# A hybrid attention layer: side work pinned behind later instructions, two down-projection tiles interleaved

## The chip, the cores and the metric

The kernel runs on one core of a Trainium2 chip. The metric is device time of one launch in microseconds (us): 954.92 us as the median of three runs before the change (954.69 to 955.83). Engines are named as in the profile: PE is TensorE (matmuls, transposes), DVE is VectorE, ACT is ScalarE, POOL is GpSimd, SP is SyncE. Here SP issues the weight loads, POOL the loads and stores of the new tokens' work, and ACT two small stores. TensorE's clock has two levels, 1.2 and 2.4 GHz; the profile shows the granted one as 0.50 and 1.00.

## The reference

One layer with 512 prompt rows and 8 new rows, which the kernel puts side by side as T = 520 columns:

```python
mod = (silu(c) @ w_ada + b_ada)            # shifts, scales and gates per sequence
h = rms_norm(x) * (1 + sc1) + sh1
q, k, v, u, vs, ga, gb = split(h @ w_in)   # 60 tiles of 128 columns
y_att = attend(rms_norm(q), rms_norm(k), v)   # prompt: dilated windows; new rows: cached keys and values
y_sgu = gelu(u) * (tril(w_s) @ layer_norm(gelu(vs)) + b_s)
x = x + g1 * ((sigmoid(ga) * (y_att @ w_pa) + sigmoid(gb) * (y_sgu @ w_ps)) @ w_out)
h2 = rms_norm(x) * (1 + sc2) + sh2
a, b = split(h2 @ w_ffn_in)                # 2 x 22 tiles of 128
x = x + g2 * ((silu(a) * b) @ w_ffn_out)   # 22 k-tiles into 8 tiles
```

Everything is float32. For a new row the scores are sums of key times query over 320 cached keys, and its output is a sum of weight times value over them.

## The kernel before

A weight tile is [128 x 1024], loaded by SP into one of five `raw` buffers, which w_ada's tiles share. `weights` (L76) splits it into a rounded part `hi` (ACT, L68) and a remainder `lo` (DVE, L69), three buffers each. A product (`mm3`, L82) takes three matmuls per k-tile, hi with the activations' high part, hi with their low part and lo with the high part (L88 to L90): 48 of 260 columns for a whole job with its two halves.

The work is a list of jobs, and `run` (L129) goes through it: weights are prepared three steps ahead, and after each job's last part `tick` advances the background tasks by one `yield`. A task's `yield n` waits n jobs. `behind(ins)` (L171) asks the scheduler to put what is written in it after the instruction `ins` in its engine's queue; all else is ordered by a scheduler with a timeline of its own, so that the text's order is not the queue's. Each engine then takes its queue in order.

The jobs: four tiles of v_sgu, four of u, then per head h three q, three k and three v tiles (36), 16 gates interleaved with 8 projections, 16 for w_out (half by half), 20 products of the first five of 22 feed-forward pairs, 17 `pair_job`s that use sums of the activations (`tt`) to save products, and 24 down-projection jobs: for each of 8 output tiles f the k-tiles 0 to 7, 8 to 15 and 16 to 21.

The tasks that the change touches:

- `constants` loads w_spatial (`wsp`) and multiplies it by the triangle on DVE (L389).
- `sample(h)` does the new rows of a head: the query row goes out to DRAM and is read back on all partitions (`qb`), keys come as `kt`, and DVE sums their products for three key groups (L689, eight per group); after the softmax the weights take the same way (`dp`, back as `pb`), the values come as `cv`, and DVE sums three, three and two rows (L732). The `kt`/`cv` tiles share two buffers, `qb`/`pb` another two.
- `attend(h)` does the prompt rows; its `x` (L600) feeds a small matmul `px` (L604) in which the two halves of a softmax meet.
- `qk_norm` scales q and k: PE spreads the row scales into a bank `rb` (L520), DVE multiplies (`n`, L522, L525), which frees the bank.
- `ada_rest` computes the later parts of `mod` from w_ada (L239, tile `ada`).
- `norm2(1)` normalises the second half after w_out, and `sums` (L905) then forms the activations' sums and splits them into `tt`.
- `divide` (L1044) splits the 22 finished products `g` into hi and lo for the down-projection, into places that come free by then: `tt`, `h2` (named h_6819 on DVE) and slots named `gh`.

Of the kernel before, what the change touches and what calls it, by code (L numbers as in the profile page):

```python
# [16 lines left out]
P = 128  # L17
# [14 lines left out]
def hybrid_layer(ctx: ExitStack, tc: tile.TileContext, io: dict):  # L32
# [43 lines left out]
    def weights(raw, n):  # L76
        hi = wp.tile([P, 1024], F32R, tag="hi", name="hi")
        lo = wp.tile([P, 1024], F32R, tag="lo", name="lo")
        split(hi[:, : n * P], lo[:, : n * P], raw[:, : n * P])
        return hi, lo  # L80

    def mm3(ps, hi, lo, xs, half, first, last):  # L82

        n = len(xs)
        cols = slice(half * HT, half * HT + HT)
        for i, (kk, xh, xl) in enumerate(xs):
            wh, wl = hi[:, kk * P : kk * P + P], lo[:, kk * P : kk * P + P]
            pe.matmul(ps, wh, xh[:, cols], start=(first and i == 0), stop=False)  # L88
            pe.matmul(ps, wh, xl[:, cols], start=False, stop=False)  # L89
            pe.matmul(ps, wl, xh[:, cols], start=False, stop=(last and i == n - 1))  # L90

    def product(hi, lo, xs, half):
        ps = bank("mm", "ps", (P, HT))
# [282 lines left out]
    def constants():  # L376
        late(qw, io["qw"])
        late(kw, io["kw"])
        late(turns, io["turns"])
        late(lnw, io["lnw"].to_broadcast([P, 512]))  # L380
        late(lnb, io["lnb"].to_broadcast([P, 512]))
        yield 1
        with behind(last_h[0]):
            dve.tensor_scalar_mul(qw, qw, float(np.float32(128.0) ** -0.5))
        late(wsp, io["wspT"])
        late(tril, io["tril"])
        yield 1
        with behind(last_h[0]):
            dve.tensor_tensor(out=wsp, in0=wsp, in1=tril.unsqueeze(1).to_broadcast([P, 8, P]), op=ALU.mult)  # L389
        late(bsp, io["bsp"])  # L390
        late(w00, io["w00"])
        yield 1
        late(bias0, io["bias0"])
        yield 1
        late(bias12, io["bias12"])
        late(n2w, io["n2w"])
# [264 lines left out]
    def sample(h):  # L661
# [23 lines left out]
        yield 3  # L685
        for g in range(3):
            rows, kt, qb = nxt.pop(0)
            for b in range(NS):
                dve.tensor_tensor_reduce(out=kt[:rows, b], in0=kt[:rows, b], in1=qb[:rows, b], scale=1.0, scalar=0.0,  # L689
                                         op0=ALU.mult, op1=ALU.add, accum_out=ssc[:rows, g, b : b + 1])  # L690
            if g == 0:
                nxt.append(keys(2))
            if g < 2:
                yield 1
# [33 lines left out]
        yield 3  # L728
        for b0 in (0, 3, 6):
            n, vt, pb = nxt.pop(0)  # L730
            for b in range(n):
                dve.tensor_tensor_reduce(out=vt[:, b], in0=vt[:, b], in1=pb[:, b], scale=1.0, scalar=0.0, op0=ALU.mult,  # L732
                                         op1=ALU.add, accum_out=ys[:, h, b0 + b : b0 + b + 1])
            if b0 == 0:
                nxt.append(vals(6))
            if b0 < 6:
                yield 1
# [26 lines left out]
    def ada_rest():  # L764
        ws = [ada_load(8, kh) for kh in range(2)]
        yield 2
        for grp in range(4, 12):
            ps = bank("t", "ada", (P, 512))
            for q in range(2):
                for kh in range(2):  # L770
                    ada_product(ps[:, q * 256 : q * 256 + 256], ws[kh], kh)
                if 2 * grp + q < 23:
                    ws = [ada_load(2 * grp + q + 1, kh) for kh in range(2)]
                if q == 0:
                    yield 1
            yield from ada_sum(ps, 4 * grp, 4)
            yield 2 if grp % 2 else 1
# [132 lines left out]
    def sums():  # L910

        early.close()
        tt = ctx.enter_context(tc.tile_pool(name="tt", bufs=1)).tile([P, 3, KD, HT], F32R, tag="tt", name="tt")
        mem["tt"] = tt
        mem["ys"] = slots("ys", "g8")
        r = [mem["ys"][0][:, 2 * j : 2 * j + 2].rearrange("p a (b c) -> p (a b) c", b=2) for j in range(4)]

        def whole(out, k0, half):
            c = slice(half * HT, half * HT + HT)
            h = h2_all[0][0].bitcast(F32)  # L920
            dve.tensor_tensor(out=out, in0=h[:, k0 : k0 + 4, c], in1=h[:, KD + k0 : KD + k0 + 4, c], op=ALU.add)

        def minus(out, a, b):
            dve.tensor_tensor(out=out, in0=a, in1=b, op=ALU.subtract)  # L924

        def halved(hi, lo, src):
            act.activation(hi, src, AF.Copy)
            minus(lo, src, hi.bitcast(F32))

        whole(r[0], 0, 0)  # L930
        whole(r[1], 4, 0)
        yield 1
        whole(r[2], 0, 1)
        minus(r[0], r[2], r[0])
        yield 1
        whole(r[3], 4, 1)
        minus(r[2], r[3], r[2])
        yield 1
        minus(r[3], r[3], r[0])
        minus(r[1], r[1], r[3])  # L940
        yield 1
        for j, src in ((0, r[3]), (1, r[2]), (2, r[1])):
            halved(tt[:, j, 0:4], tt[:, j, 4:8], src)
            yield 1
        h = h2_all[0][0]
        mem["t1"] = lambda: halved(h[:, 0:4, HT:T], h[:, KD : KD + 4, HT:T], r[0])
# [25 lines left out]
    def pair_job(i):  # L972
# [28 lines left out]
        def use(ops, after):  # L1001
            if i == NPRE:
                start_pair(i, ops)
            x, y = pend[i], slot("tr", "value", shape=(P, HT))
            g = home(i)
            a, b = bank("mm", "pa", (P, HT)), bank("mm", "pb", (P, HT))
            part(a, ops[0], 0, quarter(0, 0), True)
            if i == NPRE:
                mem["t1"]()
            dve.tensor_tensor(out=x[:, :HT], in0=a, in1=x[:, :HT], op=ALU.add)  # L1010
            yield
            part(b, ops[1], 0, quarter(0, 1), True)
            act.activation(y, b, AF.Copy)
            part(a, ops[1], 1, t_of(0), False)
            act.activation(x[:, HT:], a, AF.Copy)
            yield
            part(b, ops[2], 0, quarter(4, 1), False)
            dve.tensor_tensor(out=x[:, HT:], in0=b, in1=x[:, HT:], op=ALU.add)
            act_last[0] = act.activation(x, x, AF.Silu)
            part(a, ops[2], 1, t_of(1), False)  # L1020
            dve.tensor_tensor(out=y, in0=a, in1=y, op=ALU.add)
            if i + 1 < NFF:
                start_pair(i + 1, after)
            part(a, (own_slot("ah", i % 2), own_slot("al", i % 2)), 0, t_of(2), False)
            dve.tensor_tensor(out=g[:, :HT], in0=a, in1=x[:, :HT], op=ALU.mult)
            dve.tensor_tensor(out=g[:, HT:], in0=y, in1=x[:, HT:], op=ALU.mult)
            if i + 1 == NFF:
                divide(range(1, NFF))
            elif i + 2 == NFF:
                divide([0])  # L1030
            yield

        jobs.append(([(io["wff"][i], KD), (io["wff"][NFF + i], KD)], first, prep, use))
# [10 lines left out]
    def divide(r):  # L1044

        for k in r:
            if k == 0:
                hl = [slot("tq", "gh", F32R) for _ in range(2)]
            elif k < 7:
                t = mem["tt"][:, (k - 1) // 2].rearrange("p k c -> p (k c)")[:, (k - 1) % 2 * 2 * T : ((k - 1) % 2 + 1) * 2 * T]  # L1050
                hl = (t[:, :T], t[:, T:])
            elif k < 15:
                hl = (h2_all[0][1][k - 7], h2_all[0][1][KD + k - 7])
            elif k < 20:
                hl = [slot("pm", "gh", F32R) for _ in range(2)]
            else:
                if k == 20:
                    mem["gl"] = slots("ys", "gh", 4, F32R)[1]
                hl = mem["gl"][2 * k - 40 : 2 * k - 38]
            split(*hl, gs[k])  # L1060
            halved[k] = hl

# [9 lines left out]

    def down_job(f, k0, n):
        def fn(hi, lo):
            if k0 == 0:
                outp[f] = [bank("mm", "ps", (P, HT)) for _ in range(2)]
            for half in range(2):
                ps = outp[f][half]
                mm3(ps, hi, lo, [(k, *halved[k0 + k]) for k in range(n)], half, k0 == 0, k0 + n == NFF)
                if k0 + n == NFF:  # L1080
                    residual(xr[f], ps, xr[f], gate(1, f), half)
                    c = slice(half * HT, half * HT + HT)
                    (pool if f < 6 else sp).dma_start(out=io["o_y"][:, f, c], in_=xr[f][:, c])

        job(io["wfo"][f, :, k0 * P : (k0 + n) * P], fn, n)

    for f in range(KD):
        for k0 in range(0, NFF, KD):
            down_job(f, k0, min(KD, NFF - k0))

    run()

# [110 lines left out]
```

## Time and profile before

| | before |
|---|---|
| median of three runs | 954.92 us (954.69 to 955.83) |
| the profiled execution's own time | 951.7 us |
| its span | 949.6 us |
| PE busy | 915.8 us (96%) |
| PE weight loads busy | 873.3 us (92%) |
| DVE busy | 585.5 us (62%) |
| ACT busy | 412.3 us (43%) |
| POOL busy | 135.3 us (14%) |
| mean granted clock | 0.994 |

The profiled execution is 3.2 us (0.3%) under the median; 2.1 us of it lie outside the span. Line numbers are those of the kernel before. In a timeline a row stands for one or more like instructions in a run; its bracket gives the engine's idle time before it and what ended it. A matmul of 260 columns is shown with 0.28 us, but they are pipelined, and one starts every 0.12 us.

### The profile page before, as it was taken

To read this page: it belongs to the slowest core of one execution; us is meant where nothing else is said; L and a number is where in the kernel's file an instruction comes from. 1 tells how busy PE (TensorE), PEld (TensorE's weight loads), DVE (VectorE), ACT (ScalarE), POOL (GpSimd) and SP (SyncE) were. 2 spreads that over 40 slices of the span, in tenths; PEclk is the share of its full clock that TensorE was granted. 3 is DMA by queue.
4 is the path that set the end of the run, shared out by engine and by line. 5 is a ranking of instruction groups with operands and counts; after the bars stand their busy time and mean duration, and the time that the engine had idled before them with its cause. 6 is when DMAs were issued, how large, how long until landed. Compare 5 with 4: busy or idle time off the path is not lost.

```text
span 949.6 us, 18870 instructions
## 1 busy us (share of the span) xinstructions
PE 915.8 (96%) x7648; PEld 873.3 (92%) x7648; DVE 585.5 (62%) x1378; ACT 412.3 (43%) x802; POOL 135.3 (14%) x155
## 2 busy tenths in 40 slices
PE   4999999998999999999999999899999999899998
PEld 1799889898887999999999999899999999799998
DVE  6634575746564665753336679999887887832321
ACT  4344343542443353674323447655555555621210
POOL 0000001112102201301000322022343341000000
PEclk9999999999999999999999999999999999999999
DMA  9933536738757735735333555452332332343310
GB/s 362 369 133 117 174 114 221 266 98 272 233 176 214 249 117 156 240 120 135 100 100 96 194 187 174 159 178 90 108 116 90 116 107 84 123 111 108 111 46 23
DMA packets 43030, 146.85 MB, mean 155 GB/s; under 512 B 6456, under 2 KB 7448, under 8 KB 42944
## 3 DMA queue, kind: packets, MB, share of 16 engines
q1 hardware_dynamic: 33840, 114.34, 35.6%
q0 software_dynamic: 8608, 31.20, 11.1%
q8 instruction: 60, 0.98, 0.4%
q14 instruction: 26, 0.21, 0.1%
q10 hardware_dynamic: 496, 0.12, 0.1%
HBM read 137.01 MB, written 8.63 MB: 153 GB/s over the span
## 4 chain that ended last, share of the span: by engine, by line
PE 81%; DMA 7%; DVE 7%; issue 2%; ACT 2%; POOL 0%; DVEq 0%; POOLq 0%; ACTq 0%
PE ps L88 19%; PE ps L90 19%; PE ps L89 19%; DMA pb<-dp 4%; PE pa L953 3%; PE pa L955 3%; PE pa L954 3%; DVE lo L69 2%; PE ada L239 2%; PE pb L954 2%; PE pb L953 2%; PE pb L955 2%; PE y L648 1%; DMA wsp<-wspT 1%; PE p L954 1%
## 5 line engine op out<-in xcount | busy, mean ns | idle before, releaser
L88 PE MATMUL ps<-h,hi 128*128 128x260 f32 x1248 | 356.4, 289 | 6.1 <-ACT silu L899 2.7
L89 PE MATMUL ps<-h,hi 128*128 128x260 f32 x1248 | 355.1, 286 | 0.3 <-DVE h L277 0.3
L90 PE MATMUL ps<-h,lo 128*128 128x260 f32 x1248 | 354.3, 285 | 1.0 <-DVE lo L69 0.9
L69 DVE TENSOR_TENSOR lo<-raw,hi 128x1024 fp32r<-128x1024 f32 (+2 forms) x213 | 220.7, 1054 | 155.2 <-ACT hi L68 152.0
L68 ACT ACTIVATE hi<-raw 128x1024 fp32r<-128x1024 f32 (+2 forms) x213 | 181.3, 875 | 246.9 <-PE ps L89 217.6
L88 PEld LDWEIGHTS ps<-h,hi 128*128 128x128 f32 x1248 | 235.1, 190 | 16.9 <-issue 8.2
L90 PEld LDWEIGHTS ps<-h,lo 128*128 128x128 f32 x1248 | 236.1, 190 | 3.9 <-issue 2.1
L89 PEld LDWEIGHTS ps<-h,hi 128*128 128x128 f32 x1248 | 236.3, 189 | 3.5 <-issue 2.1
L975 POOL TENSOR_TENSOR s<-raw 128x512 f32<-128x512 f32 x17 | 34.7, 2043 | 145.7 <-DMA raw<-wff 119.3
L954 PE MATMUL pb<-h,hi 128*128 128x260 f32 x136 | 38.5, 283 | 0.4 <-DVE h L924 0.4
L953 PE MATMUL pa<-tt,hi 128*128 128x260 f32 x136 | 38.5, 283 | 0.1
L953 PE MATMUL pb<-h,hi 128*128 128x260 f32 x136 | 38.5, 283 | 0.0
L955 PE MATMUL pb<-h,lo 128*128 128x260 f32 x136 | 38.5, 283 | 0.0
L954 PE MATMUL pa<-tt,hi 128*128 128x260 f32 x136 | 38.3, 282 | 0.0
L955 PE MATMUL pa<-tt,lo 128*128 128x260 f32 x136 | 38.3, 281 | 0.0
L89 PE MATMUL ps<-gh,hi 128*128 128x260 f32 x128 | 36.3, 284 | 0.2 <-DVE gh L69 0.2
L90 PE MATMUL ps<-mh,lo 128*128 128x260 f32 x128 | 36.4, 284 | 0.0
L89 PE MATMUL ps<-ml,hi 128*128 128x260 f32 x128 | 36.3, 283 | 0.0
L88 PE MATMUL ps<-mh,hi 128*128 128x260 f32 x128 | 36.1, 282 | 0.0
L90 PE MATMUL ps<-gh,lo 128*128 128x260 f32 x128 | 36.1, 282 | 0.0
L88 PE MATMUL ps<-gh,hi 128*128 128x260 f32 x128 | 35.9, 282 | 0.0
L831 DVE SCALAR_TENSOR_TENSOR xr<-ps,mod,xr 128x260 f32<-128x260 f32 (+1 forms) x32 | 15.4, 482 | 30.9 <-PE ps L90 30.1
(271 smaller groups left out, 1886.4 us busy)
## 6 DMA issues: line engine op xcount, KB each, us to landing
raw<-win SPq DMA_DIRECT2D x60, 512.0 KB, 5.2
raw<-wff SPq DMA_DIRECT2D x54, 512.0 KB, 4.3
wada<-wada SPq DMA_DIRECT2D x48, 512.0 KB, 5.6
raw<-wout SPq DMA_DIRECT2D x16, 512.0 KB, 4.2
raw<-wfo SPq DMA_DIRECT2D x16, 512.0 KB, 4.0
kt<-ck POOLq DMA_DIRECT2D x8, 512.0 KB, 6.4
qb<-dq POOLq DMA_DIRECT2D x8, 512.0 KB, 4.9
raw<-wpj SPq DMA_DIRECT2D x8, 512.0 KB, 4.3
```

Source lines behind the costliest of these rows:

```text
L68: act.activation(hi, src, AF.Copy)
L69: return dve.tensor_tensor(out=lo, in0=src, in1=hi.bitcast(F32), op=ALU.subtract)
L88: pe.matmul(ps, wh, xh[:, cols], start=(first and i == 0), stop=False)
L89: pe.matmul(ps, wh, xl[:, cols], start=False, stop=False)
L90: pe.matmul(ps, wl, xh[:, cols], start=False, stop=(last and i == n - 1))
L239: last_ada[0] = pe.matmul(ps[32 * c : 32 * c + 32, :], cs[:, 4 * kh + c, :], w[:, c * 256 : c * 256 + 256], start=(kh == 0), stop=(kh == 1 ...
L648: pe.matmul(y[s][:, i], val, ptbs[i // 2][:, 2 * (i % 2) + e], start=((i, e - 1) not in blocks), stop=(e == 1))
L831: dve.scalar_tensor_tensor(out=dst[:, c0 : c0 + n], in0=ps[:, :n], scalar=g[:, 0:1], in1=x[:, c0 : c0 + n], op0=ALU.mult, op1=ALU.add)
L953: pe.matmul(ps, hi[:, c], xh, start=(first and k == 0), stop=False, skip_group_check=True)
L954: pe.matmul(ps, hi[:, c], xl, start=False, stop=False, skip_group_check=True)
L955: pe.matmul(ps, lo[:, c], xh, start=False, stop=(k == 3), skip_group_check=True)
L975: pool.tensor_tensor(out=own_slot("s1", i % 2)[:, :512], in0=b[:, :512], in1=b[:, 512:], op=ALU.add)
```

## The change

It adds and removes no instruction; only the order in the queues differs.

- `last_lo` is the latest weight tile's `lo` split in the text's order, which, as weights are prepared three steps ahead, belongs to a later job; `last_mm` is the latest product's last matmul.
- The mask of `wsp`, each group of key sums, each group of value sums and each of the 11 steps of `sums` go behind `last_lo`. The mask waits two jobs more, and `sums` takes one step per job instead of five bundles.
- Each ada product goes behind `last_mm`.
- `divide` is spread: k = 0 and 1 at the pair jobs 19 and 20, 2 to 7 in three places of the last pair job, 8 to 21 in the first two down jobs of f = 0 behind `last_lo`. The places shift by one.
- The two multiplications that finish a pair swap their order, and the down jobs of f = 0 and f = 1 alternate.

```diff
-        split(hi[:, : n * P], lo[:, : n * P], raw[:, : n * P])
+        last_lo[0] = split(hi[:, : n * P], lo[:, : n * P], raw[:, : n * P])
...
-            pe.matmul(ps, wl, xh[:, cols], start=False, stop=(last and i == n - 1))
+            last_mm[0] = pe.matmul(ps, wl, xh[:, cols], start=False, stop=(last and i == n - 1))
...
-        yield 1
-        with behind(last_h[0]):
+        yield 3
+        with behind(last_lo[0]):
             dve.tensor_tensor(out=wsp, in0=wsp, in1=tril.unsqueeze(1).to_broadcast([P, 8, P]), op=ALU.mult)
...
-            for b in range(NS):
-                dve.tensor_tensor_reduce(out=kt[:rows, b], in0=kt[:rows, b], in1=qb[:rows, b], scale=1.0, scalar=0.0,
...
+            with behind(last_lo[0]):
+                for b in range(NS):
+                    dve.tensor_tensor_reduce(out=kt[:rows, b], in0=kt[:rows, b], in1=qb[:rows, b], scale=1.0,
...
-            for b in range(n):
-                dve.tensor_tensor_reduce(out=vt[:, b], in0=vt[:, b], in1=pb[:, b], scale=1.0, scalar=0.0, op0=ALU.mult,
...
+            with behind(last_lo[0]):
+                for b in range(n):
...
-                for kh in range(2):
-                    ada_product(ps[:, q * 256 : q * 256 + 256], ws[kh], kh)
+                with behind(last_mm[0]):
+                    for kh in range(2):
+                        ada_product(ps[:, q * 256 : q * 256 + 256], ws[kh], kh)
...
+        todo = [lambda: whole(r[0], 0, 0), lambda: whole(r[1], 4, 0), lambda: whole(r[2], 0, 1),
...
+        todo += [lambda j=j: halved(tt[:, j, 0:4], tt[:, j, 4:8], r[3 - j]) for j in range(3)]
+        for step in todo:
+            with behind(last_lo[0]):
+                step()
             yield 1
...
+            if i + 1 == NFF:
+                with behind(out):
+                    divide((2, 3))
...
+            if i + 1 == NFF:
+                with behind(out):
+                    divide((4, 5))
...
-            dve.tensor_tensor(out=g[:, :HT], in0=a, in1=x[:, :HT], op=ALU.mult)
             dve.tensor_tensor(out=g[:, HT:], in0=y, in1=x[:, HT:], op=ALU.mult)
-            if i + 1 == NFF:
-                divide(range(1, NFF))
+            out = dve.tensor_tensor(out=g[:, :HT], in0=a, in1=x[:, :HT], op=ALU.mult)
+            if i + 3 == NFF:
+                divide([0])
             elif i + 2 == NFF:
-                divide([0])
+                divide([1])
+            elif i + 1 == NFF:
+                with behind(out):
+                    divide(range(6, 8))
...
+            if f == 0 and k0 + KD < NFF:
+                with behind(last_lo[0]):
+                    divide(range(k0 + KD, min(k0 + 2 * KD, NFF)))
...
-    for f in range(KD):
-        for k0 in range(0, NFF, KD):
-            down_job(f, k0, min(KD, NFF - k0))
+    order_ = [(f, k0) for k0 in range(0, NFF, KD) for f in range(2)]
+    order_ += [(f, k0) for f in range(2, KD) for k0 in range(0, NFF, KD)]
+    for f, k0 in order_:
+        down_job(f, k0, min(KD, NFF - k0))
```

What the queues hold now is shown at three places, all on DVE. The first is around the last value sums of head 0 (`cv,yss<-cv,pb`, each followed by a row that reads its accumulator), before:

```order
L507 SCALAR_TENSOR_TENSOR rl<-rs,low,rh 96x520
L510 TENSOR_TENSOR rls<-rl,own 96x24
L732 ISA cv,yss<-cv,pb 128x320
L732 ISA yss 128x1
L732 ISA cv,yss<-cv,pb 128x320
L732 ISA yss 128x1
L742 TENSOR_TENSOR yss<-yss,vsr 128x8
L69 TENSOR_TENSOR lo<-raw,hi 128x1024
L522 SCALAR_TENSOR_TENSOR n<-z,kw,rb 128x512
L525 SCALAR_TENSOR_TENSOR n<-z,kw,rb 128x512
```
and after the change, where L737 is the value sums, L525 and L528 are `n`, L674 is a small product of the new rows:

```order
L525 SCALAR_TENSOR_TENSOR n<-z,kw,rb 128x512
L531 SCALAR_TENSOR_TENSOR ks<-z,kw,rsm 128x8 x3
L528 SCALAR_TENSOR_TENSOR n<-z,kw,rb 128x512
L674 TENSOR_TENSOR qkp<-qs,ks 128x24
L528 SCALAR_TENSOR_TENSOR n<-z,kw,rb 128x512
L69 TENSOR_TENSOR lo<-raw,hi 128x1024
L737 ISA cv,yss<-cv,pb 128x320
L737 ISA yss 128x1
L737 ISA cv,yss<-cv,pb 128x320
L737 ISA yss 128x1
```
The last sums stood ahead of a weight split and of the three `n`; now the `n` come first, then the split, then the sums.

The second place is at the key sums of head 1. `xo` and `so` belong to the first softmax of the prompt rows, `p`, `nm` and `x` to the second, `M` and `e` to their merging. Before, the first eight sums stood directly ahead of these rows (they are not shown), and the second group begins with the last row:

```order
L606 TENSOR_TENSOR xo_2872<-px,turns 128x32
L608 TENSOR_REDUCE so_2874<-xo_2872 128x4x2
L69 TENSOR_TENSOR lo<-raw,hi 128x1024
L589 ISA p_2745,st_2748<-sc,bias_598 128x256
L589 ISA st_2748 128x1
L589 ISA p_2746,st_2748<-sc,bias_598 128x256
L589 ISA st_2748 128x1
L592 TENSOR_SCALAR nm_2750<-st_2748 128x4
L616 TENSOR_TENSOR M_3080<-st_2748,so_2874 128x4
L617 TENSOR_TENSOR e_3081<-st_2748,M_3080 128x4
L618 TENSOR_TENSOR e_3081<-so_2874,M_3080 128x4
L689 ISA kt,ssc<-kt,qb 128x128
```
After the change the first eight sums stand between a split and these rows:

```order
L609 TENSOR_TENSOR xo_2872<-px,turns 128x32
L592 ISA p_2745,st_2748<-sc,bias_598 128x256
L592 ISA st_2748 128x1
L592 ISA p_2746,st_2748<-sc,bias_598 128x256
L592 ISA st_2748 128x1
L611 TENSOR_REDUCE so_2874<-xo_2872 128x4x2
L566 COPY v<-vtp 128x512
L595 TENSOR_SCALAR nm_2750<-st_2748 128x4
L619 TENSOR_TENSOR M_3080<-st_2748,so_2874 128x4
L620 TENSOR_TENSOR e_3081<-st_2748,M_3080 128x4
L621 TENSOR_TENSOR e_3081<-so_2874,M_3080 128x4
L603 TENSOR_TENSOR x_2895<-st_2748,turns 128x32
```
The split that came third is now ahead of the first key sums, and the second group of key sums, which stood ahead of `x`, is no longer there.

The third place is the end of the last pair job: L1021 completes one of its terms, L1026 and L1025 finish its product g, the last L1025 being also what frees the bank `pa`. Before:

```order
L1021 TENSOR_TENSOR value<-pa,value 128x260
L69 TENSOR_TENSOR h_6819<-g_7371,h_6819 128x520
L69 TENSOR_TENSOR gh<-g_7371,gh 128x520
L69 TENSOR_TENSOR tt<-g,tt 128x520 x2
L69 TENSOR_TENSOR lo<-raw,hi 128x768
L69 TENSOR_TENSOR gh<-g_7371,gh 128x520
L1026 TENSOR_TENSOR g<-value,gate 128x260
L69 TENSOR_TENSOR tt<-g,tt 128x520
L1025 TENSOR_TENSOR g<-pa,gate 128x260
L69 TENSOR_TENSOR tt<-g,tt 128x520
L69 TENSOR_TENSOR gh<-g,gh 128x520 x4
L69 TENSOR_TENSOR lo<-raw,hi 128x1024 x2
```
After the change, where L1023, L1030 and L1031 are the same three:

```order
L1023 TENSOR_TENSOR value<-pa,value 128x260
L69 TENSOR_TENSOR tt<-g,tt 128x520 x2
L1030 TENSOR_TENSOR g<-value,gate 128x260
L69 TENSOR_TENSOR lo<-raw,hi 128x1024
L69 TENSOR_TENSOR h_6819<-g,h_6819 128x520 x2
L69 TENSOR_TENSOR h_6819<-g_7371,h_6819 128x520 x6
L1031 TENSOR_TENSOR g<-pa,gate 128x260
L69 TENSOR_TENSOR tt<-g,tt 128x520 x2
L69 TENSOR_TENSOR lo<-raw,hi 128x1024
L69 TENSOR_TENSOR lo<-raw,hi 128x768
L69 TENSOR_TENSOR gh<-g_7371,gh 128x520 x2
L69 TENSOR_TENSOR gh<-g,gh 128x520 x4
```
Between L1030 and L1031, where one split into `tt` stood, there are now a weight split and eight splits into h_6819; the `gh` splits come later.

## Rows read from the trace of the kernel before

**Rows 1.** page, part 1: engine, busy us, share of the span, instructions.

```profile
PE 915.8 (96%) x7648; PEld 873.3 (92%) x7648; DVE 585.5 (62%) x1378; ACT 412.3 (43%) x802; POOL 135.3 (14%) x155
```

**Rows 2.** TensorE's waits: line, what it waited for: us in total, times, longest.

```profile
PE rb L520 <- DVE n L522: 2.9, 1, 2.9
...
PE ps L88 <- ACT silu L899: 2.7, 1, 2.7
...
PE ps L89 <- DVE tt L69: 2.4, 2, 1.7
...
PE vtp L561 <- DVE xo L606: 1.2, 1, 1.2
...
PE ada L239 <- DMA wada<-wada: 1.0, 1, 1.0
...
PE ps L90 <- DVE lo L69: 0.9, 2, 0.6
...
PE ps L88 <- ACT tt L68: 0.8, 1, 0.8
...
PE pa L953 <- DVE value L1021: 0.5, 1, 0.5
...
PE rb L520 <- DVE yss L742: 0.4, 1, 0.4
```

**Rows 3.** TensorE by stretch: stretch, us, busy us (instructions), granted clock, DMA share, GB/s.

```profile
54.40:57.80 3.40, 3.40 (x18) 0.50 0.80 233
231.90:235.30 3.40, 3.40 (x15) 0.50 1.01 388
242.30:245.70 3.40, 3.40 (x29) 1.00 0.87 228
598.00:601.40 3.40, 0.85 (x8) 1.00 0.73 253
```

**Rows 4.** TensorE timeline, one wait: start, us, engine, line, operation [idle before <-releaser].

```profile
598.56 0.28 PE L90 MATMUL ps<-h,lo 128*128 128x260 f32 x1
601.57 0.39 PE L88 MATMUL ps<-h,hi 128*128 128x260 f32 x1 [2.73 <-ACT silu L899]
```

**Rows 5.** VectorE timeline at the spatial mask.

```profile
51.43 1.23 DVE L389 TENSOR_TENSOR wsp<-wsp,tril 128x1024 f32<-128x1024 f32 x1 [2.07 <-DMA wsp<-wspT]
```

**Rows 6.** timelines of GpSimd and VectorE at the value sums of head 0.

```profile
218.63 0.71 POOL L724 DMA_DIRECT2D pb<-dp  x1
...
227.88 0.49 DVE L732 CUSTOM_DVE_ANT_0 cv<-cv,pb 128x320 f32<-128x320 f32 x1 [4.89 <-DMA pb<-dp]
...
228.94 1.23 DVE L69 TENSOR_TENSOR lo<-raw,hi 128x1024 fp32r<-128x1024 f32 x1
230.08 0.74 DVE L522 SCALAR_TENSOR_TENSOR n<-z,kw,rb 128x512 f32<-128x512 f32 x1
```

**Rows 7.** timelines of ScalarE, VectorE and TensorE at the key sums of head 1.

```profile
237.51 0.27 ACT L668 ACTIVATE qrow<-qrow 24x128 f32<-24x128 f32 x1 [2.10 <-PE qrow L666]
...
247.70 0.29 DVE L689 CUSTOM_DVE_ANT_0 kt<-kt,qb 128x128 f32<-128x128 f32 x1 [4.38 <-DMA qb<-dq]
...
249.40 0.19 DVE L606 TENSOR_TENSOR xo<-px,turns 128x32 f32<-128x32 f32 x1
...
254.39 0.18 DVE L600 TENSOR_TENSOR x<-st,turns 128x32 f32<-128x32 f32 x1
...
255.22 0.30 PE L604 MATMUL px<-x,turns 128*128 128x32 f32 x2
```

**Rows 8.** VectorE timeline at the value sums of head 1.

```profile
294.88 0.49 DVE L732 CUSTOM_DVE_ANT_0 cv<-cv,pb 128x320 f32<-128x320 f32 x1 [1.47 <-DMA pb<-dp]
```

**Rows 9.** VectorE timeline after the last w_out job.

```profile
586.21 1.23 DVE L921 TENSOR_TENSOR g<-h 128x1040 f32<-128x1040 f32 x1
```

**Rows 10.** VectorE timeline in the last pair job.

```profile
814.89 1.91 DVE L69 TENSOR_TENSOR h<-g,h 128x520 fp32r<-128x520 f32 x3
...
821.92 0.42 DVE L1025 TENSOR_TENSOR g<-pa,gate 128x260 f32<-128x260 f32 x1
```

More of the change, by code (lines that the diff above doesn't have):

```diff
@@ L78, in weights @@
         lo = wp.tile([P, 1024], F32R, tag="lo", name="lo")
-        split(hi[:, : n * P], lo[:, : n * P], raw[:, : n * P])
+        last_lo[0] = split(hi[:, : n * P], lo[:, : n * P], raw[:, : n * P])
         return hi, lo
+    last_lo, last_mm = [None], [None]
     def mm3(ps, hi, lo, xs, half, first, last):
@@ L687, in sample @@
             rows, kt, qb = nxt.pop(0)
-            for b in range(NS):
-                dve.tensor_tensor_reduce(out=kt[:rows, b], in0=kt[:rows, b], in1=qb[:rows, b], scale=1.0, scalar=0.0,
-                                         op0=ALU.mult, op1=ALU.add, accum_out=ssc[:rows, g, b : b + 1])
+            with behind(last_lo[0]):
+                for b in range(NS):
+                    dve.tensor_tensor_reduce(out=kt[:rows, b], in0=kt[:rows, b], in1=qb[:rows, b], scale=1.0,
+                                             scalar=0.0, op0=ALU.mult, op1=ALU.add, accum_out=ssc[:rows, g, b : b + 1])
             if g == 0:
@@ L730, in sample @@
             n, vt, pb = nxt.pop(0)
-            for b in range(n):
-                dve.tensor_tensor_reduce(out=vt[:, b], in0=vt[:, b], in1=pb[:, b], scale=1.0, scalar=0.0, op0=ALU.mult,
-                                         op1=ALU.add, accum_out=ys[:, h, b0 + b : b0 + b + 1])
+            with behind(last_lo[0]):
+                for b in range(n):
+                    dve.tensor_tensor_reduce(out=vt[:, b], in0=vt[:, b], in1=pb[:, b], scale=1.0, scalar=0.0,
+                                             op0=ALU.mult, op1=ALU.add, accum_out=ys[:, h, b0 + b : b0 + b + 1])
             if b0 == 0:
@@ L928, in halved @@
             minus(lo, src, hi.bitcast(F32))
[L930 to L943, printed above, removed]
+        todo = [lambda: whole(r[0], 0, 0), lambda: whole(r[1], 4, 0), lambda: whole(r[2], 0, 1),
+                lambda: minus(r[0], r[2], r[0]), lambda: whole(r[3], 4, 1), lambda: minus(r[2], r[3], r[2]),
+                lambda: minus(r[3], r[3], r[0]), lambda: minus(r[1], r[1], r[3])]
+        todo += [lambda j=j: halved(tt[:, j, 0:4], tt[:, j, 4:8], r[3 - j]) for j in range(3)]
+        for step in todo:
+            with behind(last_lo[0]):
+                step()
             yield 1
@@ L1017, in use @@
             part(b, ops[2], 0, quarter(4, 1), False)
-            dve.tensor_tensor(out=x[:, HT:], in0=b, in1=x[:, HT:], op=ALU.add)
+            out = dve.tensor_tensor(out=x[:, HT:], in0=b, in1=x[:, HT:], op=ALU.add)
+            if i + 1 == NFF:
+                with behind(out):
+                    divide((2, 3))
             act_last[0] = act.activation(x, x, AF.Silu)
             part(a, ops[2], 1, t_of(1), False)
-            dve.tensor_tensor(out=y, in0=a, in1=y, op=ALU.add)
+            out = dve.tensor_tensor(out=y, in0=a, in1=y, op=ALU.add)
+            if i + 1 == NFF:
+                with behind(out):
+                    divide((4, 5))
             if i + 1 < NFF:
@@ L1046, in divide @@
         for k in r:
-            if k == 0:
+            if k < 2:
                 hl = [slot("tq", "gh", F32R) for _ in range(2)]
-            elif k < 7:
-                t = mem["tt"][:, (k - 1) // 2].rearrange("p k c -> p (k c)")[:, (k - 1) % 2 * 2 * T : ((k - 1) % 2 + 1) * 2 * T]
+            elif k < 8:
+                t = mem["tt"][:, (k - 2) // 2].rearrange("p k c -> p (k c)")[:, k % 2 * 2 * T : (k % 2 + 1) * 2 * T]
                 hl = (t[:, :T], t[:, T:])
-            elif k < 15:
-                hl = (h2_all[0][1][k - 7], h2_all[0][1][KD + k - 7])
-            elif k < 20:
+            elif k < 16:
+                hl = (h2_all[0][1][k - 8], h2_all[0][1][k])
+            elif k < 21:
                 hl = [slot("pm", "gh", F32R) for _ in range(2)]
             else:
-                if k == 20:
-                    mem["gl"] = slots("ys", "gh", 4, F32R)[1]
-                hl = mem["gl"][2 * k - 40 : 2 * k - 38]
+                hl = slots("ys", "gh", 2, F32R)[1]
             split(*hl, gs[k])
```

## The prediction

> **What bounds the kernel now.** I read the engines' shares first: PE is busy for 915.8 of 949.6 us, every other engine far less [rows 1]. So the time is PE's queue, and a change that neither adds nor removes an instruction can win only what PE lacks, 949.6 - 915.8 = 33.8 us, and what PE does at a lower clock. Second I read what PE waited for. The reader is to see no steady loss but single waits, nearly each with another releaser; the nine rows that the change may reach add up to 12.8 us [rows 2]. Third I read PE stretch by stretch with its granted clock, because a wait can cost more than its length: at 231.9 us, right behind the 2.9 us wait for `n`, the clock is at its lower level, 1.2 GHz, and PE starts 15 instructions in 3.4 us where it starts 29 at the upper level [rows 3]. Half of that stretch, 1.7 us, is lost on top. Then I went to each wait in the timelines and asked whether the new order still has what caused it.
>
> One correction: matmuls overlap, so a wait costs a little more than its idle time. The last matmul before the wait for the silu starts at 598.56, the next at 601.57: 3.01 us where 0.12 is normal, so 2.9 lost for 2.73 shown [rows 4]. I add 0.15 to each wait that goes.
>
> **The change part by part.**
>
> *Mask (A).* DVE idles 2.07 us for the DMA of `wsp` at the head of its queue [rows 5]; a weight split behind it comes late, and PE waits the shorter of the two waits in the row of `lo` L69, 0.9 - 0.6 = 0.3 us [rows 2]. Two jobs later the DMA has landed. Gain 0.3 + 0.15, about 0.5. The low clock at 54.4 us [rows 3] follows these waits, but other waits stay beside this one, so I count nothing for it; the low end of the range has its 1.7.
>
> *Value sums (B).* For head 0 the third `pb` load is issued at 218.63, and DVE stands 4.89 us before its sums at 227.88; behind them in the queue are the split at 228.94 and `n` at 230.08, which frees the bank that PE wants [rows 6]. In the new order the `n` and a split come ahead of those sums. The first sums come one split later, about 1.1 us, so the load is issued at about 219.7 and, with the same 9.2 us, lands at about 229; DVE reaches the sums only after three `n` (0.74 us the first, the others not shorter) and a split of 1.23, at about 230. The wait goes: 2.9 + 0.15. So does the low clock behind it, 1.7. Gain 4.8, between 0 (the wait stays in another place) and 4.8.
>
> *Key sums (C).* For head 1 the wait of `vtp` for `xo`, 1.2 us [rows 2], is due to eight sums of 1.70 us (247.70 to 249.40) that stood on the DMA for 4.38 us [rows 7]. The bank that `vtp` needs is freed by ACT in the new order. But these sums stay ahead of `x`, which PE needs for `px`. From the query row's copy at 237.51 to the first sum are 10.2 us [rows 7], the sums 1.7, and what remains to `x` I estimate at 4.2: in the rows, 249.40 to 254.39 are 5.0, of which a split of some 1.2 and the second group of sums, 1.7, go; the four exponentials and the copy into `v` are what is in their way. So `x` is there about 16 us after the query row, or 253.6 by the clock of before. PE reaches `px` 255.22 - 237.51 = 17.7 us after it, less the 1.2 of the removed wait and 5 matmuls that now stand elsewhere (0.6): 15.9. That is a new wait of about 0.3, which I round to 0.5 for the exponentials' uncertainty, from 0 to 3 over the heads. Gain 1.35 - 0.5 = 0.85, of which I keep 0.5, since head 3 has the same order with less distance; range -2 to 1.4.
>
> *Ada products (D).* PE waited 1.0 us for a `wada` tile [rows 2]. Its raw buffer came free late because a split stood behind value sums of head 1 that waited 1.47 us for their load [rows 8]; the split is now ahead of the sums. That product stands where it stood in PE's queue. Gain 1.0 + 0.15, about 1.2; range 0 to 1.5.
>
> *Head 2 (E).* The wait of `rb` for the value sums' total, 0.4 [rows 2], goes in the same way: 0.5; range 0 to 1.
>
> *Sums of the activations (F).* The wait for the silu, 2.7 us [rows 2], is the end of a chain: after the last w_out job DVE runs the first sum of 1.23 us [rows 9] ahead of the residual's last piece, so the square sum, the mean, the logarithm on ACT and its table load are all late, and ACT changes its table for the silu only then. In the new order the sum is behind a later split, the total stands 36 rows earlier in PE's queue and the second square ahead of the weight's rounding on ACT. The 1.23 us go directly, the rest by the shorter queue on ACT. I keep 0.6 of the wait: gain 2.9 - 0.6 = 2.3; range 0.9 to 2.9.
>
> *Divide and the order of the down jobs (G).* At the end of the last pair DVE runs 21 splits without a break, and PE waits for tt twice (2.4), for a rounded tt (0.8) and for `value` (0.5) [rows 2]: 3.7, and with 0.15 for each of four 4.3. Now two tiles alternate, so that the first needs only eight products at the start. But the new queue has eight h_6819 splits and a weight split between L1030 and L1031, and L1031 frees `pa`, the bank for the second output tile. One such split is 0.61 back to back: three from 814.89 take 1.91, the last one's end of 0.08 overlapping the next [rows 10]. L1030 and L1031 are 0.34 (0.42 less the overlap) and the weight split 1.15 [rows 6, 10]. From the end of `value` the queue has 2 x 0.61 + 0.34 + 1.15 + 8 x 0.61 + 0.34 = 7.9 us to the end of L1031. In before `value` came behind the three splits, at 816.7; with two earlier ones ahead of it I place its end 1.1 before that, at 815.6. So the bank is free at about 823.5. Counting PE's matmuls at 0.12 each without its waits, it is there at about 820.9, an estimate. New wait 2.6, gain 4.3 - 2.6 = 1.7; range 0 to 4.3.
>
> Sum: 0.5 + 4.8 + 0.5 + 1.2 + 0.5 + 2.3 + 1.7 = 11.5. Work pinned in some 40 places also comes later everywhere else, and PE's slack there is of the size of the waits that the rows show as small, 0.4 to 0.5 each [rows 2]; for two of these I take 1.0 off. 951.7 - 10.5 = 941.2 us for the profiled execution. It stood 3.2 under the median of the runs, so the forecast is 944.4 us.
>
> **Two rules weighed.** The low clock of rows 3 follows the wait of 2.9 us, but during and behind the wait of 2.73 at 598 the clock stays at its upper level [rows 3, 4]. The Trainium skill ("TensorE: Matmul & The Clock Gate", section "HAM oscillation — how this bites in real kernels") has long idle gaps drop the clock and the next work start cold; that agrees at 231.9 and does not at 598. By the rule applied to both, F would give 1.7 more, by the row nothing.
>
> A load issued by POOL took 9.2 us for `pb` while DVE worked [rows 6]. The Trainium skill ("SBUF — State Buffer", the box on the "DVE blocks DMA" trap) says that POOL must write a load's descriptors itself and is locked out by some DVE operations. By it, loads could land still later where DVE is now fuller ahead of the sums; the next paragraph's first rival has the price.
>
> **The rivals.**
> 1. *The DMA wait moves.* The sums still stand in DVE's one queue and everything behind them waits. If the third `pb` lands 2 us after 230 instead of 1 us before, the split or the copy of `v` behind the sums is late and PE waits as before. For: 9.2 us from issue to landing, and the issue comes later [rows 6]. Against: what PE needs first, `n`, is ahead now. B and D then give nothing: 941.2 + 4.8 + 1.2 = 947.2, and 950.4 by the median. Chance 0.13.
> 2. *All of it goes.* The bank at the last pair is free in time (G 4.3), `px` does not wait (C 1.4), the silu's wait goes wholly (F 2.9), nothing comes off for small waits, and the low clock at 54.4 goes too: 10.5 + 2.6 + 0.9 + 0.6 + 1.0 + 1.7 = 17.3, so 937.6. For: the new waits that I subtract are estimates from queues, which no row shows. Against: the eight splits do stand ahead of L1031. Chance 0.14.
> 3. *Slower: key sums ahead of `x`.* If the query rows come back as late as 10.2 us for each head [rows 7] and the sums behind a split start 2 us later than I have them, `px` waits 3 us in heads 1 to 3 and the clock falls each time, 1.7 more: 14.1 us. It decides once the waits of the three heads together exceed 10.5 + 0.5 us. 941.2 + 0.5 + 14.1 = 955.8, or 959 by the median. For: nothing else is between the sums and `x`. Against: in before `x` had 6.7 us from the first sum, and now 5.9. Chance 0.07.
> 4. *It cancels.* B's and G's gains are lost to waits of like size, and C, D, E give nothing: 0.5 + 2.3 - 1.0 = 1.8, so 953.1. Chance 0.07.
>
> That the change doesn't reach the queues is excluded by the three places shown: the rows there did move.
>
> **How the numbers follow.** The forecast has 0.59, the rivals 0.13, 0.14, 0.07 and 0.07. The forecast's own range, from one or two of the ends of B, C, F and G, is 941 to 948. The range for 8 in 10 takes in rivals 1 and the near part of 2, and leaves out the rest of 2, rivals 3 and 4: 939 to 952. A measurement of this kernel tells no change to about 0.2%, 1.9 us. Faster by more: forecast, 1 and 2, 0.86; within: 0.07; slower: 0.07.
>
> **What would show it.** The PE waits for `n`, `xo`, `wada` and the value total are not in the new profile (B, C, D, E), and at 232 us PE's clock is at its upper level. The wait for the silu is under 1 us (F). At about 821 PE waits some 2.6 us for L1031 (G); if it waits for another releaser or not at all, that step was wrong. A wait of `px` above 1 us, or DVE waiting for `pb` with PE behind it, would make the forecast wrong.

## The result, and the profile after

The changed kernel takes 939.11 us (median of four runs, 938.87 to 939.98), the kernel before 955.38 beside it (954.69 to 956.12): a ratio of 0.983, 95% interval 0.981 to 0.985. The forecast was 944.4 with a range of 939 to 952; the time is inside, at its very edge. The profiled execution takes 938.87 us, its span is 936.7, against 951.7 and 949.6.

PE's share in the page's first part answers to [rows 1]:

```profile
PE 910.1 (97%) x7648; PEld 870.7 (93%) x7648; DVE 585.3 (62%) x1378; ACT 413.1 (44%) x802; POOL 136.0 (15%) x155
```

The same matmuls, 12.9 us less span and 5.7 us less busy time. Some 3.4 of the 5.7 are the clock (an estimate: three low stretches of 3.4 us before, one after, each costing half its length); what the other 2.3 are isn't shown. What PE waited for, to be read against [rows 2] (line, releaser: us in total, times, longest; lines have moved by 3 to 6):

```profile
PE ps L91 <- DVE g L1031: 2.5, 1, 2.5
...
PE pb L953 <- DVE h L930: 1.8, 1, 1.8
...
PE px L607 <- DVE e L624: 0.9, 1, 0.9
PE ada L242 <- DMA wada<-wada: 0.8, 1, 0.8
PE ps L93 <- DVE lo L69: 0.6, 1, 0.6
```

Seven of the nine rows of before have no successor; the w_ada wait shown here is an early one, at 36 us, where the profile of before has none, and the one at 306 is gone. Two more rows are new, L1031 and `px`, and both are in the prediction. `h` L930 is not: it has grown from this row of before, which the prediction did not look at:

```profile
PE pb L954 <- DVE h L924: 0.4, 1, 0.4
```

The granted clock by stretch, against [rows 3] (stretch, us, busy us and instructions, clock, DMA share, GB/s), with one more stretch of before first:

```profile
27.10:30.50 3.40, 3.40 (x22) 0.50 1.03 414
```

and after the change:

```profile
27.10:30.50 3.40, 3.40 (x34) 1.00 1.03 416
54.40:57.80 3.40, 3.40 (x31) 1.00 0.92 274
223.00:226.40 3.40, 3.40 (x30) 1.00 0.86 242
633.90:637.30 3.40, 3.40 (x16) 0.52 0.54 178
813.40:816.80 3.40, 3.40 (x28) 1.00 0.00 0
```

The low stretches behind the start, the mask and the value sums (231.9 before, now around 223) are gone; one has come at 633.9, behind the grown wait for `h`. The longer wait at 813 has none behind it.

### The profile page after: what moved, and what is told of

Its sections match the earlier page's. It is cut to its first block, busy times and chain, and to the rows that moved or that the text cites. A ratio compares the mean times of both kernels' runs of the same rounds, so it can differ in the third digit from the quotient of the medians.

```text
span 936.7 us, 18863 instructions
## 1 busy us (share of the span) xinstructions
PE 910.1 (97%) x7648; PEld 870.7 (93%) x7648; DVE 585.3 (62%) x1378; ACT 413.1 (44%) x802; POOL 136.0 (15%) x155
```

## Experiments

All but the repeat undo or add one part. "Before" is the kernel before on the same chip; its median was 954.1, 954.5 and 955.7 in three groups of runs. Every ratio is against the one of its own group.

**Mask, key and value sums alone** (the rest as before):

```diff
-        yield 1
-        with behind(last_h[0]):
+        yield 3
+        with behind(last_lo[0]):
             dve.tensor_tensor(out=wsp, in0=wsp, in1=tril.unsqueeze(1).to_broadcast([P, 8, P]), op=ALU.mult)
...
+            with behind(last_lo[0]):
+                for b in range(NS):
...
+            with behind(last_lo[0]):
+                for b in range(n):
```

> The kernel before with one part of the change: the mask, the key sums and the value sums go behind the latest weight split; ada products, sums of activations, divide and the down jobs stay as before. Theory (the gain is the sum of the waits that went, with the low-clock stretches behind them): the mask 0.5, the low clock at 27 and 54 us 1.7 each, value and key sums with their low clock about 5.5, the two small waits behind them 1.7, in all 11 of the 16 us: about 944.5. Rival (the gain of the parts is not their sum, because early waits only move): under 6 us, above 949.

943.81 us, ratio 0.987 (0.984 to 0.991): some 10 us, as the theory had it. In its view of PE's waits `n` and `xo` have no row, and the w_ada tile has 0.2 us left:

```profile
PE ps L91 <- ACT silu L905: 2.7, 1, 2.7
PE ps L92 <- DVE tt L69: 2.4, 2, 1.7
...
PE px L607 <- DVE e L624: 0.9, 1, 0.9
...
PE px L607 <- DVE x L603: 0.6, 1, 0.6
```

The `px` rows are the price: it waits in two heads.

**The mask alone** (only the first of these edits):

> The kernel before with the mask alone moved. Theory: its PE wait of 0.3 to 0.5 us goes, and if the low clock at 54 us hangs on that wait, 1.7 more: 952.9 to 954.9. Rival: what the timed runs of the kernel before have above its profiled one (3 to 4 us) is due to low clock in this early stretch; then the mask alone brings 3 to 4 us, 951 to 952.

954.15 us against 954.07, ratio 0.999 (0.996 to 1.002): no change that can be told. The rival, 3 to 4 us, lies at or beyond the end of the interval (3.6 us less); whether the theory's half microsecond is there these runs can't say. The traces say more of its second part, the low clock at 54 us. In the mask's profile it is gone:

```profile
54.40:57.80 3.40, 3.40 (x31) 1.00 0.77 254
```

It is there in all six profiles with the mask in its old place (the kernel before, value sums, key sums, one job later, activations' sums, divide) and in none of the seven with the mask moved. So it hangs on the wait at the mask; why the twelve timed runs show no gain for it is open.

**Value sums alone, key sums alone** (one `with behind(last_lo[0]):` each):

> The kernel before with the value sums alone behind the latest weight split. Theory (the prediction's steps B, D and E): the waits of rb for n, of the w_ada tile and of rb for the value total go, with the low clock behind the first: 6.5 less. Rival (mask, keys and values hold each other's waits up, and one alone only hands the wait on to the next sums): under 4 less.

> The kernel before with the key sums alone behind the latest weight split. Theory (step C): the wait of vtp for xo (1.2 to 3.3 in the profiles) goes, a wait of px of about 0.9 comes: 0.5 to 2.5 less. Rival: nothing, since value sums of the head before still stand on their loads ahead of it.

Values: 948.64, ratio 0.993 (0.991 to 0.996), 7 us by the medians, 4 to 9 by the interval; keys: 953.07, 0.997 (0.994 to 0.999), 2.6 us, 1 to 5 by the interval. Both agree with the theory within these intervals, the keys at the upper end of its range, and by the medians the two and the mask add up to the 10 of the first experiment. So the value sums carry most of it. In the traces the waits named are gone (of w_ada the one at 306), but the parts are not independent: with the key sums alone `px` doesn't wait at all, and with the value sums alone it waits in three heads:

```profile
PE px L607 <- DVE e L624: 3.2, 3, 1.9
```

**One job later, without a pin:**

```diff
         nxt = [keys(0), keys(1)]
-        yield 3
+        yield 4
...
         nxt = [vals(0), vals(3)]
-        yield 3
+        yield 4
```

> The kernel before, with key and value sums waiting one job more (yield 4 for 3) and no pin at all; nothing else changed. Theory (it matters only that the loads have landed when VectorE reaches the sums): most of what the pins of mask, keys and values bring, 5 to 8 us less than the kernel before, with a smaller spread. Rival (the place right behind a weight split matters, so that splits and multiplications that TensorE needs are not behind sums): under 3 us less.

955.98 us, ratio 1.002 (1.000 to 1.004). My theory falls. Its view of the tile `pb` shows that DVE still stands on these loads (who waited: us, times), and its view of PE's waits that `x` is now late:

```profile
  DVE cv L737: 19.3, 9
```

```profile
PE px L607 <- DVE x L603: 4.6, 2, 3.1
```

In the kernel before, the first row reads:

```profile
  DVE cv L732: 24.4, 9
```

A later place in the text is not a later place in the queue: the scheduler orders the queue, and nine groups of sums stand again where their loads had not landed. In the changed kernel the view of `pb` (a bank of the pair jobs has the same name) has no row for the sums at all:

```profile
  ACT gate L1021: 19.8, 15
  ACT value L1012: 2.6, 1
  DVE gate L1017: 0.2, 1
```

**The activations' sums alone** (the list of single steps, each `behind(last_lo[0])`):

> The kernel before with the 11 single steps of the activations' sums behind the latest weight split, nothing else moved. Theory: the silu's wait of 2.7 us goes (2.9), and the wait for the split named h at the first pair job grows from 0.4 to 1.8 us and brings low clock (1.4 + 1.7): no change within 0.5, about 955. Rival: the larger wait at the first pair comes from other parts of the change; then 952.5.

954.08 us, ratio 0.999 (0.996 to 1.001): no change that can be told, as the theory said, but the rival's 952.5 lies inside the interval too. The trace tells them apart in one point: the silu's wait is gone, and with these steps alone this one has come, so it doesn't come from other parts of the change. PE's timeline, and the clock behind it:

```profile
646.96 0.39 PE L953 MATMUL pb<-h,hi 128*128 128x260 f32 x1 [1.86 <-DVE h L930]
```

```profile
647.00:650.40 3.40, 3.40 (x28) 1.00 0.51 175
```

The low clock that the theory put behind it is not in this profile.

**Divide and the order of the down jobs alone:**

> The kernel before with the spread divide, the alternating first two down tiles and the swapped multiplications, nothing else moved. Theory: waits of 4.3 at the end of the last pair become one of 2.5 on the second finishing multiplication: gain 2 to 2.6, about 953. Rival: the gain at this place in the changed kernel came from the earlier arrival of other work; then no change, 955 to 956.

952.03 us, ratio 0.996 (0.993 to 0.999): 2 us by the medians. The waits for `tt` and `value` are gone, and PE's timeline has one in their place:

```profile
828.86 0.54 PE L91 MATMUL ps<-gh,hi 128*128 128x260 f32 x1 [2.50 <-DVE g L1038]
```

Here the clock is low behind it, which it is not behind the same wait in the changed kernel:

```profile
829.10:832.50 3.40, 3.40 (x17) 0.52 0.00 0
```

The pin of the ada products was not run: the program built without it is the same as the one with it, so nothing hangs on it.

**The changed kernel again, and three versions of it.**

> The changed kernel itself, on the same chip as the next three. Theory: 939, with a spread over its runs of 2 us against more than 10 in the kernel before, since the waits whose length hangs on a DMA are gone.

```diff
-            out = dve.tensor_tensor(out=g[:, :HT], in0=a, in1=x[:, :HT], op=ALU.mult)
+            out = mem["out"] = dve.tensor_tensor(out=g[:, :HT], in0=a, in1=x[:, :HT], op=ALU.mult)
...
-                with behind(last_lo[0]):
+                with behind(mem["out"] if k0 == 0 else last_lo[0]):
                     divide(range(k0 + KD, min(k0 + 2 * KD, NFF)))
```

> The changed kernel, with the second group of divide (k = 8 to 15) behind the last finishing multiplication instead of behind the weight split, so that the bank is freed ahead of the eight splits into h2. Theory: the wait of 2.5 us on that multiplication goes to under 0.5: 2 to 2.6 less than the changed kernel. Rival: the splits k = 6 to 15 are then what is late for the next tiles, and PE waits as long for them: no change within 0.5.

```diff
-        mem["t1"] = lambda: halved(h[:, 0:4, HT:T], h[:, KD : KD + 4, HT:T], r[0])
+        mem["t1"] = lambda: [halved(h[:, a : a + 1, HT:T], h[:, KD + a : KD + a + 1, HT:T], r[0][:, a : a + 1])
+                             for a in range(4)]
```

> As fix_out, and the split of the activations' sum at the first pair job (into h2) in four pieces, three of which come ahead of the last weight split there. Theory: the wait of 1.8 us goes, and with it the low clock behind it: 3 to 3.6 less than fix_out, so 5 to 6 less than the changed kernel. Rival: the low clock has another cause; then 1.5 to 2 less than fix_out.

> As the version with the split into h2 in four pieces, but in two, one of which comes ahead of the last weight split there. Theory: the waits there (0.3 and 0.9) stay or shrink by a few tenths: within 1 us of the version in four pieces, 934 to 936. Rival: with fewer pieces VectorE and ScalarE are done sooner and the 0.9 for the next finishing addition goes: 1 to 2 less.

The repeat took 938.62 us (937.2 to 939.1). With the bank freed ahead of the eight splits: 935.82 (934.5 to 936.8), and the row of L1031 is gone from the waits, with nothing in its place there: 2.8 us less, the theory's 2 to 2.6 within the spread. The four pieces on top: 935.08 (934.6 to 936.5), 0.7 and not 3 less, so the theory falls and the rival's 1.5 to 2 are not reached either. Of the wait of 1.8 us 0.3 are left, but the pieces push the next finishing addition back, for which PE then waits 0.9 us. Two pieces: 933.89 (933.3 to 936.0), the best time here, ratio 0.978 (0.975 to 0.981), with these rows for that place in its view of PE's waits:

```profile
PE pa L953 <- DVE gate L1010: 0.5, 1, 0.5
PE pb L954 <- DVE h L930: 0.5, 2, 0.2
```

That is 1.2 under the four pieces by the medians, but the runs of the two overlap and stem from different groups; whether two are better than four stays open. All runs of the three versions are under every run of the changed kernel.

## Why the prediction was right, and where it was short

*Value sums (B): right.* DVE after the change, against [rows 6] (start, us, engine, line, operation, idle before and its end):

```profile
222.67 0.74 DVE L525 SCALAR_TENSOR_TENSOR n<-z,kw,rb 128x512 f32<-128x512 f32 x1
...
226.47 1.15 DVE L528 SCALAR_TENSOR_TENSOR n<-z,kw,rb 128x512 f32<-128x512 f32 x1 [1.53 <-PE rb L523]
227.54 1.21 DVE L69 TENSOR_TENSOR lo<-raw,hi 128x1024 fp32r<-128x1024 f32 x1
228.67 0.48 DVE L737 CUSTOM_DVE_ANT_0 cv<-cv,pb 128x320 f32<-128x320 f32 x1
```

It is now DVE that waits for PE at `n`, and the sums start without any wait. The 4.8 us of B and the 1.7 of D and E are 6.5; the value sums alone brought 7. One reading was off: the prediction has DVE working during the 9.2 us of the `pb` load, but for 4.89 of them it stood idle [rows 6], so they show nothing of DVE holding the load up.

*Key sums (C): right in kind.* The first key sums of head 1 still stand on their load, and `px` waits 0.9, where I had 0.5 against [rows 7]; DVE's timeline and PE's:

```profile
242.72 0.29 DVE L693 CUSTOM_DVE_ANT_0 kt<-kt,qb 128x128 f32<-128x128 f32 x1 [3.77 <-DMA qb<-dq]
...
248.27 0.19 DVE L603 TENSOR_TENSOR x<-st,turns 128x32 f32<-128x32 f32 x1 [1.85 <-ACT p L599]
```

```profile
248.60 0.38 PE L607 MATMUL px<-x,turns 128*128 128x32 f32 x2 [0.93 <-DVE e L624]
```

What `x` waits for now is ACT's exponentials (1.85 us), as the prediction had it. I sized C at 0.5; alone it measured 2.6 (1 to 5). The wait that it removes varies: `vtp` waited 1.2 us for `xo` in the trace I had, 2.0 and 3.3 in the profiles of the mask alone and of divide alone, and not at all in that of the activations' sums alone, all three with the heads worked as in before.

*Sums of the activations (F): a step was missing.* I had 0.6 of the silu's wait left; nothing is. But I followed only the first sum and not the last: the split L930 into h2, which overwrites h2 and so can't start before PE has read it, stands behind splits for the pairs and a multiplication, and its wait grows from the 0.4 of before to 1.8. In DVE's timeline:

```profile
632.24 0.42 DVE L908 TENSOR_TENSOR g<-ps,silu 128x260 f32<-128x260 f32 x1
632.58 1.23 DVE L930 TENSOR_TENSOR h<-g,h 128x1040 fp32r<-128x1040 f32 x1
```

So most of what the silu's wait gave is taken back here, and the steps alone bring nothing that can be told. The two pieces show it from the other side.

*Divide (G): right.* A new wait of 2.6 was forecast, for L1031 and behind eight splits; it is 2.46. DVE's timeline, against [rows 10], and PE's:

```profile
806.21 0.42 DVE L1030 TENSOR_TENSOR g<-value,gate 128x260 f32<-128x260 f32 x1
806.87 1.22 DVE L69 TENSOR_TENSOR lo<-raw,hi 128x1024 fp32r<-128x1024 f32 x1 [0.24 <-ACT hi L68]
808.01 4.96 DVE L69 TENSOR_TENSOR h<-g,h 128x520 fp32r<-128x520 f32 x8
812.89 0.42 DVE L1031 TENSOR_TENSOR g<-pa,gate 128x260 f32<-128x260 f32 x1
```

```profile
813.37 0.39 PE L91 MATMUL ps<-gh,hi 128*128 128x260 f32 x1 [2.46 <-DVE g L1031]
```

*Where the other 6 us came from.* The forecast was 10.5 us for the profiled execution and the measured span is 12.9 less. Two low-clock stretches are not in this profile (2 x 1.7): one at 54 us, which I had left standing and which belongs to the mask, and one at 27, which I had not looked at. That second one looks like luck: the waits ahead of it (0.5, 0.3 and 0.6 us) are the same in both profiles. The 0.6 that I took off for F did not come; L930 takes back 1.4 and a stretch of its own. Of the 1.0 for small waits about half came (0.8 at 36 us and 0.3 at `adat`, against some 0.7 of small waits gone). Together that is about 12. So the time is nearer to rival 2 (937.6) than to the forecast: of that rival's terms the silu's whole wait and the stretch at 54 us came, while the bank and `px` are late as forecast.

The rest, some 3.4 us of the 16 between the medians, is the step "it stood 3.2 under the median of the runs", which I carried over to the new kernel. It belongs to the kernel before: that one's profiled run was a lucky one, and the changed one's stands at its median (938.87 and 939.11). The mean clock doesn't explain that luck: at 0.994 it is the mean of the runs. Its waits were in part short ones: `rb` waited 0.2 us for `yat`, and 0.9 to 1.1 in the profiles of the mask, the keys, the activations' sums and divide alone; how much of the 3 us that is stays open.

Over 64 runs the kernel before takes 949.5 to 962.0 us, and about half of that spread goes with its mean granted clock (0.990 to 0.998): 1.07 us more per thousandth less, correlation -0.74. A thousandth of the span is 0.95 us, so this is about what the slower clock costs by itself. The changed kernel's eight runs take 937.2 to 940.0, with clocks of 0.995 to 1.000. The mean clock rose from 0.994 to 0.997: by this slope some 3 of the 16 us are clock (an estimate), of which the prediction has 1.7, in B.

What a wait does to the clock no single row tells. The Trainium skill ("TensorE: Matmul & The Clock Gate", section "HAM oscillation — how this bites in real kernels") has long idle gaps bring the low clock. The traces here agree for some gaps and not for others of the same length: the wait of 1.80 us at 633.86 is followed by 0.52, but in the repeat of the very same kernel the same wait is not (its PE timeline, and its clock by stretch):

```profile
633.75 0.39 PE L953 MATMUL pb<-h,hi 128*128 128x260 f32 x1 [1.73 <-DVE h L930]
```

```profile
633.00:636.40 3.40, 2.65 (x21) 1.00 0.35 96
```

Over all profiles: the wait for `h` (1.7 to 1.9 us) is followed by a low stretch in two of four, the one for the second finishing multiplication (2.5) in one of three, and the silu's (2.73) in five of seven; the kernel before and the mask alone are the two where it is not. With one job later:

```profile
603.14 0.39 PE L91 MATMUL ps<-h,hi 128*128 128x260 f32 x1 [2.73 <-ACT silu L905]
```

```profile
603.90:607.30 3.40, 3.40 (x19) 0.53 0.47 148
```

So each such wait is a chance of losing 1.7 us more, and the kernel with fewer waits is the faster and the steadier one here. The prediction counted that part for B alone. For F it went by the one row and took nothing, where five of seven profiles have 1.7. For the mask it had the low stretch in its rows and left 1.7 out, since other waits stay beside that one; they do stay (0.46 and 0.48 us), and the stretch is gone.

## What to carry to other kernels

Where one engine is 96% busy, read its waits one by one and ask what stands ahead of the releaser in the releaser's queue: an instruction on a load at a queue's head holds up all behind it, and binding it behind a named instruction moved it, while a later place in the text did not. Follow every instruction that such a move delays to its last reader, here the last split and not the first sum. Whether a wait brings the low clock is read from several profiles, not from one. Compare distributions over runs, not one profile with a median: the offset between them belongs to one kernel and is not carried over.

## What the runs showed of the hardware

A split of 128 x 512 on DVE takes 0.68 us, but two of them took 3.49 while POOL worked on tiles of the same size beside them. The changed kernel's timelines of POOL and of DVE:

```profile
625.18 1.29 POOL L974 TENSOR_TENSOR s<-raw 128x512 f32<-128x512 f32 x1 [2.45 <-DMA raw<-wff]
626.54 1.61 POOL L975 TENSOR_TENSOR raw<-raw 128x512 f32<-128x512 f32 x1
```

```profile
625.22 3.49 DVE L69 TENSOR_TENSOR lo<-raw,hi 128x512 fp32r<-128x512 f32 x2
...
630.44 0.68 DVE L69 TENSOR_TENSOR lo<-s,hi 128x512 fp32r<-128x512 f32 x1
```

From 625.2 to 628.1 POOL is busy, and DVE's splits last 1.75 each on average. It goes the other way too: from 659.33 a POOL addition lasts 2.82 us while DVE's splits beside it keep their 0.68. The Trainium skill ("SBUF — State Buffer", the box on the "DVE blocks DMA" trap) speaks of a port that DVE and GpSimd share and from which DVE can lock GpSimd out; the rows fit that, with each of the two slowed in turn. No run here parted them, so it is not shown to be the cause.
